# Rope by one copy and four transfers, a later split of the meta columns, and output weights placed earlier, in a hybrid attention layer

## The chip, the cores and the metric

The kernel runs on one core of a Trainium2 chip. The metric is the device time of one execution in microseconds (us), median of several runs. The core has five engines that each work through an instruction queue of their own in order: PE (TensorE, the matmuls; its weight loads are shown as PEld), DVE (VectorE), ACT (ScalarE), POOL (GpSimd) and SP (SyncE). In this kernel SP issues nearly all DMA transfers. An engine waits for another through semaphores.

## The reference

One decoder layer, float32, on 2048 tokens of width 1024 with 16 learned meta tokens ahead of them. Two attention branches run side by side on the same normalised input.

```python
xn = rms_norm(h, norm_gain[l])
proj = xn @ w_in[l]
sb_q, sb_k, sb_v, sw_q, sw_k, sw_v, sb_z, sw_z, g_sb, g_sw = jnp.split(proj, offsets, axis=-1)
o_sb = stick_breaking_attention(sb_q, sb_k, sb_v, valid)          # 8 heads of 64
q = rope(sw_q, pos)                                               # 16 heads of 64
k = rope(sw_k, pos)                                               # 2 heads of 64
o_sw = sliding_window_sink_attention(q, k, sw_v, attn_sinks[l], valid)   # window 128
y_sb = (o_sb * jax.nn.silu(sb_z)) @ w_branch_sb[l]
y_sw = (o_sw * jax.nn.silu(sw_z)) @ w_branch_swa[l]
merged = jax.nn.sigmoid(g_sb) * y_sb + jax.nn.sigmoid(g_sw) * y_sw
h = h + merged @ w_out[l]
return rms_norm(h, final_norm_gain)[:, BLOCK:]
```

The shapes of the heads are left out. `rope` takes each head's 64 values as two halves x1 and x2 and returns x1·cos − x2·sin and x2·cos + x1·sin: each half needs its partner half, 32 positions away.

## The kernel before

**Layout and splitting.** Activations lie transposed: features on the 128 partitions, tokens along the row in groups of 512 (four groups). To keep float32 accuracy each operand of a projection is held as a high and a low part, and a product is three matmuls (L461: xh·wh, xl·wh, xh·wl); a tile of 128 features by 512 tokens is 24 such matmuls over the eight 128-rows of the depth. The low part of a weight tile is `wl`, a subtraction on DVE (L119), stored to memory for the second use of the same weights by SP (`l_in_w_in<-wl`).

**Stages.** The work runs in two halves, groups 2 and 3 and then groups 0 and 1. In the profile the first sliding-window stage lies at about 60 to 372 us, the first stick-breaking stage at 372 to 562 us, a stage of gate products at 562 to 776 us, the second sliding-window stage at 776 to 1080 us, the second stick-breaking stage at 1080 to 1600 us, and `finish` (branch projections, merge, output projection, last norm) from 1600 us to the end.

**Who sets the order.** PE's instructions run in the order in which the program writes them: `weave` mixes the projection tiles with the units of attention by a clock of estimated costs. The other engines and SP are ordered by a scheduler from its own timeline, except in a hand-ordered stretch at the start, which ends at `hand.close()`.

**The sliding-window stage.** `window` builds key tiles (`sw_k`, L687 and L689 spread them over `kk`), value tiles (`sw_v`) and query tiles (`sw_q`). A key or query tile that comes out of PE in a PSUM bank goes through `rope` (L675 to L679): ACT copies each 32 rows to the place of their partner rows (four activations of 32x512, lines 675 and 676, `u`); DVE multiplies the bank itself by the cosines (L677, `t`), then `u` by the sines (L678), and adds (L679). A query tile is then split into high and low parts (`put_q`: casts on ACT at L736, subtractions on DVE at L737). One attention unit is: scores on PE (L756), copies and masks (L759, L760), maximum (L762), exponentials (L764), scaling (L765, L766); three units later the weights are transposed on PE (L790), split into `ph` (ACT) and `pl` (DVE) by `evac_split` (L126, L127), POOL selects `pm` from both (L796), PE multiplies with the values (L812), and ACT and DVE write the output (L814, L818). Value differences `xs` are moved between partitions with 64 KB transfers inside the core (`xs<-xs`). Every tile named `tmp` comes from one ring of nine.

**The stick-breaking stage.** `row` makes a row of scores (L915), a sigmoid (L918) and a running product (L923, L925); `turn` transposes rows (L944). POOL gathers the last 16 columns, those of the meta tokens, in `mr` (L931), and ACT and DVE split them into `m` (L934, L935), which `turn_meta` uses later.

**Finish.** `out_weights(k, ch)` loads a 128x512 piece of the output weights (`a<-in_w_out`), and splits it (L269 on ACT, L270 on DVE) into two tiles of the ring `ringr`, which has 32. The first column half (`ch` 0) is made inside the loop over `d`, piece `d` at the end of step `d`; the second half is made while the output products (L333 to L335) run.

Of the kernel before, what the change touches and what calls it, by code (L numbers as in the profile page):

```python
# [8 lines left out]
F32R = mybir.dt.float32r  # L9
I32 = mybir.dt.int32  # L10
AF = mybir.ActivationFunctionType
ALU = mybir.AluOpType
# [4 lines left out]
P = 128  # L17
# [3 lines left out]
NM = 16  # L21
GT = 512
# [21 lines left out]
def f32(ap):  # L44
    return ap.bitcast(F32)
# [3 lines left out]
def tile_kernel(ctx, tc, x, xt, meta, metat, gain, w_in, w_sb, w_sw, w_out, sinks, fgain,  # L49
# [8 lines left out]
    def DMA(dst, src):  # L58
        nc.sync.dma_start(*(t.bitcast(F32) if t.dtype == F32R else t for t in (dst, src)))
# [47 lines left out]
    msd = [dram(f"msd{p}", [NM, P]) for p in range(2)]  # L107
    vsv = dram("vsv", [P, 2 * P], F32R)

    vsplit, hsplit = [False], [True]  # L110

    def split(h, l, src):

# [121 lines left out]
    def finish(ringl, osw, first):  # L235
# [4 lines left out]
            return ps("gzt"[next(banks) % 3])  # L240

        def ringr(dt=F32R):
            return cp.tile([P, GT], dt, tag="R", name="ringr", bufs=32)

        def small(tag, bufs):
            return cp.tile([P, GT], F32, tag=tag, name=tag, bufs=bufs)
# [15 lines left out]
        for half, groups in enumerate(halves):  # L262
# [12 lines left out]
            for d, g in order:  # L275
                if d == 3 and g == groups[0]:
                    osb = {(k, g): gated(od, zs, k, g, ringr, lambda: small("a", AB)) for g in groups for k in range(4)}
                if d not in ws_of:
                    ws_of[d] = first if half == d == 0 else weights(d * P, w_sw)
                ws = ws_of[d]  # L280
                acc = bank()
                project(acc, ws, [osw[k, g] for k in range(8)])
                gt = small("gt", 3)
                DMA(gt, gw[d][g])
                part[d, g] = ringr(F32)
                V.tensor_tensor(part[d, g], acc, gt, op=ALU.mult)
            for d in range(8):
                ws = weights(d * P, w_sb)
                for g in groups:
                    acc = bank()  # L290
                    project(acc, ws, [osb[k, g] for k in range(4)])
                    gt = small("gt", 3)
                    DMA(gt, gs[d][g])
                    V.tensor_tensor(gt, acc, gt, op=ALU.mult)
                    V.tensor_tensor(gt, gt, part[d, g], op=ALU.add)  # L295
                    mh, ml = merged[d, g] = ringl(), ringl()
                    A.copy(mh, gt)  # L297
                    V.tensor_tensor(ml, gt, f32(mh), op=ALU.subtract)
                out_weights(d, 0)
            for g in groups:  # L300
                for t0 in range(0, 4, 2):
                    res, ssq, scaled_by = {}, {}, {}
# [82 lines left out]
            tp.tile(shape, F32, tag=tag, name=tag, bufs=n)  # L385

    def tmp(dt=F32, rows=P):
        return tp.tile([rows, GT], dt, tag="tmp", name="tmp", bufs=9)

    def ring_x(dt=F32):  # L390
        return tp.tile([P, GT], dt, tag="xs", name="xs", bufs=XS)
# [256 lines left out]
    def window(half, groups, sp):  # L648
# [22 lines left out]

        def rope(acc, c, s, t, u, scale):

            for o in range(0, P, 64):
                A.activation(u[o:o + 32], acc[o + 32:o + 64], AF.Copy, scale=scale)  # L675
                A.activation(u[o + 32:o + 64], acc[o:o + 32], AF.Copy, scale=scale)
            V.scalar_tensor_tensor(t, acc, scale, c, op0=ALU.mult, op1=ALU.mult)  # L677
            V.tensor_tensor(u, u, s, op=ALU.mult)  # L678
            V.tensor_tensor(t, t, u, op=ALU.add)  # L679

# [169 lines left out]
    def stick(groups, bp):  # L850
# [45 lines left out]
        def row(h, g, n, j):  # L896

            if n == j == 0:
                load_kv(h, g)
                state[h, g] = {"q": load_q(h, g), "last": {}}  # L900
            st = state[h, g]
            last = st["last"]
            b0 = 4 * (g + n) + j
            nb = min(4, NB - b0)
            end = b0 + nb == NB
            w = nb * P + (NM if end and nb < 4 else 0)
            k0 = (b0 - 4 * groups[0]) * P
            pieces = [("z", 0, w)]
            if end and nb == 4:
                pieces = [("z", 0, w // 2), ("z", w // 2, w // 2 + NM)]  # L910
                w += NM
            banks = [ps(tag) for tag, _, _ in pieces]
            for t, qt in enumerate(st["q"]):
                for z, (_, c, m) in zip(banks, pieces):
                    T.matmul(z[:, :m], lhsT=qt[:, j * P:(j + 1) * P], rhs=kt[h][:, k0 + c:k0 + c + m], start=t == 0, stop=t == 1)  # L915
            r = bp.tile([P, RW], F32, tag="row", name="row", bufs=12)
            for z, (_, c, m) in zip(banks, pieces):
                A.activation(r[:, c:c + m], z[:, :m], AF.Sigmoid, scale=-1.0)  # L918
            if n == 0 and mask is None:
                G.affine_select(out=r[:, :P], in_=r[:, :P], pattern=[[1, P]], compare_op=ALU.is_ge,  # L920
                                fill=1.0, base=-1, channel_multiplier=-1)
            if n == 0 and mask is not None:
                V.tensor_tensor_scan(r[:, :w], r[:, :w], mask[:, :w], 1.0, op0=ALU.mult, op1=ALU.max)  # L923
            else:
                V.tensor_tensor_scan(r[:, :w], r[:, :w], r[:, :w], last[j] if n else 1.0, op0=ALU.mult, op1=ALU.min)  # L925
            last[j] = r[:, w - 1:w]
            rows_of[h, g, n, j] = r
            if end:
                if j == 0:
                    st["mr"] = bp.tile([P, 4, NM], F32, tag="mr", name="mr", bufs=2)  # L930
                G.tensor_copy(st["mr"][:, j], r[:, w - NM:w])  # L931
                if j == 3:
                    m = st["m"] = bp.tile([P, 4, 2, NM], F32R, tag="m", name="m", bufs=2)
                    A.copy(m[:, :, 0], st["mr"])  # L934
                    V.tensor_tensor(m[:, :, 1], st["mr"], f32(m[:, :, 0]), op=ALU.subtract)  # L935

        def turn(h, g, n, i):

            i = 3 - i if n == 0 else i
            nr = i + 1 if n == 0 else 4  # L940
            tr = ps("t")
            for j in range(nr):
                k0 = (i - j) % 4 * P
                T.transpose(tr[:, j * P:(j + 1) * P], rows_of[h, g, n - (j > i), j][:, k0:k0 + P], ident)  # L944
            m = nr * P
            wh = bp.tile([P, GT], F32R, tag="wh", name="wth", bufs=3)
            wl = bp.tile([P, GT], F32R, tag="wl", name="wtl", bufs=3)
            evac_split(wh[:, :m], wl[:, :m], tr[:, :m])
            av_todo.append((h, g, vc[h, g + n][:, i, :], wh[:, :m], wl[:, :m], n == 0 and i == 3, False))

        def turn_meta(h, g):
            p, a = divmod(h, 2)
# [31 lines left out]
        for s in range(n + lt + 3):  # L984
            if s < n:
                row(*steps[s])
                yield 0.45 if s >= lt else 1.31
            t = s - lt
            if 0 <= t < n:
                turn(*steps[t])  # L990
                turned.append(s)
                yield 0.43
                h, g, step, i = steps[t]
                if g + step == 3 and i == 1:
                    turn_meta(h, g)
                    yield 0.11
                if g + step == i == 3:
                    av_todo.append((h, g, vm[:, h // 2, h % 2, :], wm[g % 2], None, False, True))
                    turned.append(s)
            while av_todo and turned[0] < s - 1:  # L1000
                del turned[0]
                yield values()
# [341 lines left out]
    for half, groups in enumerate(halves):  # L1344
        gts = [lambda spec=spec: gate(*spec) for spec in specs[half]]
        with tc.tile_pool(name=f"swa{half}", bufs=1, side="left") as sp:
# [19 lines left out]
            if m:  # L1366
                (wk, use_k, _), (wv, use_v, _), (wq, use_q, _) = sw_k(), sw_v(), sw_q(0)
                hold[0] = True
                drain(col_tile(wk, g0, use_k), col_tile(wv, g0, use_v), col_tile(wq, g0, use_q, bank="z"))
                flush(waiting)  # L1370
                drain(lagged(col_tile(wk, g1, use_k, True, "o", "t")))
                hold[0] = False
                meta_k = pending[:]
                del pending[:]
                drain(col_tile(wv, g1, use_v, True, "z", "t"))
                pending.append(lambda: flush(waiting))
                back = tp.tile([P, GT], F32, tag="rb", name="back", bufs=1)
                for i in range(2):
                    sums_back.append(back[:NM, i * P:(i + 1) * P])
                    DMA(sums_back[i], msd[i])  # L1380
                hand.close()
                vsplit[0] = False
                drain(tiles_by_tile(q[0][1:], groups[:1]))
                vsplit[0] = True
                late.extend(meta_k)
                pending.append(lambda: pending.extend(held))
            else:
                for mk, gs_ in ((sw_k, groups), (sw_v, groups), *((f, groups[:1]) for f in q[0])):
                    w, use, _ = mk()
                    for g in gs_:  # L1390
                        drain(lagged(col_tile(w, g, use, bank=("g", "z")[len(begun) % 2])))
                        begun.append(g)
# [120 lines left out]
```

## Time and profile before

| | |
|---|---|
| three runs, us | 2091.18, 2091.21, 2091.5 (median 2091.21) |
| the profiled execution, its own time | 2093.26 us |
| its span in the profile | 2091.2 us |
| granted clock of TensorE | 0.999 |
| instructions | 30957 |

The profile is of one execution. The page gives for each engine its busy time and how many instructions it ran. A row of the view of groups reads: line, engine, operation, output<-input, shape and count, then busy time, mean ns of one, and the idle time of the engine just before these instructions with what ended it. A row of the waits reads: engine, output, line <- what ended the wait, then us in total, times, and the longest. A row of the timeline reads: start, duration, engine, line, operation, tiles, shape, and in brackets the idle time before it with its releaser; neighbours of one kind are joined (x2, x4). A row of stages reads: from and to, length, then busy time and count of PE, PEld, DVE, ACT and POOL, the granted clock, the busy share of the DMA engines, and GB/s.

### The profile page before, as it was taken

How to read it: one execution, taken by the hardware profiler on the slowest of the kernel's cores; microseconds unless marked ns; L12 is line 12 of the kernel's file. 1: busy time of each engine (PE TensorE's matmuls, PEld its weight loads, DVE VectorE, ACT ScalarE, POOL GpSimd, SP SyncE). 2: the span in 40 equal slices, each digit the busy share in tenths (PEclk: the TensorE clock that was granted, in tenths of full speed). 3: DMA queues.
4: the chain of work that ended last, by engine and by line, in shares of the span. 5: the costliest groups of instructions: out<-in, count | busy, mean ns of one | idle time of the engine just before them, and what ended most of it. 6: DMA issues, size and time to landing. Idle time of an engine off the chain costs nothing.

```text
span 2091.2 us, 30957 instructions
## 1 busy us (share of the span) xinstructions
PE 2075.8 (99%) x10579; PEld 1743.0 (83%) x10579; DVE 1461.4 (70%) x2383; ACT 1091.0 (52%) x2657; POOL 343.5 (16%) x682
## 2 busy tenths in 40 slices
PE   9999999999999999999999999999999999999998
PEld 7888888888888888888888888888888888788887
DVE  7897986877687754888728888777774547464553
ACT  6677774577665335777735555655653202320121
POOL 1233444331000000333310000000000343000000
PEclk9999999999999999999999999999999999999999
DMA  9855545866287574435455444343424986568522
GB/s 335 323 187 195 192 171 181 253 201 185 87 291 292 201 257 154 159 131 172 151 176 161 120 131 128 113 131 94 125 84 168 359 303 219 186 228 303 154 96 91
DMA packets 170094, 391.48 MB, mean 187 GB/s; under 512 B 23728, under 2 KB 28208, under 8 KB 169936
## 3 DMA queue, kind: packets, MB, share of 16 engines
q1 hardware_dynamic: 169648, 389.23, 55.5%
q8 instruction: 84, 1.38, 0.3%
q14 instruction: 74, 0.61, 0.1%
q10 hardware_dynamic: 288, 0.27, 0.0%
HBM read 241.68 MB, written 145.18 MB: 185 GB/s over the span
## 4 chain that ended last, share of the span: by engine, by line
PE 90%; DVE 4%; ACT 3%; DMA 1%; issue 1%; POOL 1%; SPq 0%; DVEq 0%; ACTq 0%; POOLq 0%
PE ps_g L461 39%; PE ps_o L970 6%; PE ps_z L915 6%; PE ps_t L944 6%; PE ps_z L756 3%; PE ps_o L812 2%; PE ps_g L259 1%; PE ps_g L260 1%; PE ps_g L258 1%; PE ps_t L790 1%; PE ps_z L260 1%; PE ps_z L259 1%; PE ps_z L258 1%; PE ps_t L259 1%; PE ps_t L260 1%; PE ps_t L258 1%
## 5 line engine op out<-in xcount | busy, mean ns | idle before, releaser
L461 PE MATMUL ps_g<-xh,wh 128*128 128x512 f32 x1264 | 516.1, 408 | 0.8 <-DVE tmp L677 0.6
L461 PE MATMUL ps_g<-xl,wh 128*128 128x512 f32 x1264 | 495.1, 392 | 0.7 <-DVE xl L1192 0.6
L461 PE MATMUL ps_g<-xh,wl 128*128 128x512 f32 x1264 | 494.9, 392 | 0.4 <-DVE wl L119 0.4
L925 DVE TENSOR_TENSOR_SCAN row<-row 128x512 f32<-128x512 f32 (+4 forms) x256 | 290.2, 1134 | 116.1 <-POOL row L920 60.0
L461 PEld LDWEIGHTS ps_g<-xh,wl 128*128 128x128 f32 x1264 | 237.3, 188 | 53.3 <-DVE wl L119 0.8
L461 PEld LDWEIGHTS ps_g<-xh,wh 128*128 128x128 f32 x1264 | 238.1, 188 | 39.4 <-ACT xh L1191 1.2
L461 PEld LDWEIGHTS ps_g<-xl,wh 128*128 128x128 f32 x1264 | 238.6, 189 | 38.3 <-DVE xl L1192 2.0
L918 ACT ACTIVATE row<-ps_z 128x512 f32<-128x512 f32 (+4 forms) x352 | 174.8, 508 | 159.5 <-PE ps_z L915 155.1
L127 DVE SCALAR_TENSOR_TENSOR wtl<-ps_t,wth 128x512 fp32r<-128x512 f32 (+1 forms) x320 | 188.8, 590 | 21.3 <-ACT wth L126 20.7
L126 ACT ACTIVATE wth<-ps_t 128x512 fp32r<-128x512 f32 (+1 forms) x320 | 171.6, 536 | 61.6 <-PE ps_t L944 59.8
L915 PE MATMUL ps_z<-kt,q 128*128 128x512 f32 (+4 forms) x704 | 183.6, 349 | 2.2 <-ACT row L918 2.2
L944 PE MATMUL ps_t<-ident,row 128*128 128x128 f32 x1088 | 171.4, 273 | 1.0 <-DVE wtl L127 0.8
L944 PEld LDWEIGHTS ps_t<-ident,row 128*128 128x128 f32 x1088 | 134.6, 140 | 33.0 <-DVE wtl L127 1.8
L915 PEld LDWEIGHTS ps_z<-kt,q 128*128 128x128 f32 x704 | 124.4, 188 | 27.6 <-ACT row L918 5.3
L970 PE MATMUL ps_o<-wth,vc 128*128 128x512 f32 (+1 forms) x320 | 131.3, 410 | 0.0
L970 PE MATMUL ps_o<-wtl,vc 128*128 128x512 f32 (+1 forms) x320 | 116.4, 364 | 0.0
L764 ACT ACTIVATE sc<-sc,nm 128x129 f32<-128x129 f32 x256 | 100.0, 393 | 29.9 <-DVE nm L762 29.1
L931 POOL COPY mr<-row 128x16 f32<-128x16 f32 x128 | 28.3, 223 | 444.6 <-DVE row L925 401.9
L612 ACT ACTIVATE tmp<-ps_g 128x512 f32<-128x512 f32 x80 | 47.9, 599 | 83.6 <-PE ps_g L461 77.3
L297 ACT CAST ringl<-gt 128x512 fp32r<-128x512 f32 x32 | 19.9, 622 | 128.5 <-DVE gt L295 127.6
L117 POOL TENSOR_SCALAR wh<-raw 128x1024 fp32r<-128x1024 f32 (+1 forms) x45 | 50.2, 1116 | 215.7 <-PE ps_g L461 49.8
L923 DVE TENSOR_TENSOR_SCAN row<-row,mask 128x512 f32<-128x512 f32 (+2 forms) x64 | 70.0, 1100 | 17.7 <-ACT row L918 17.1
(442 smaller groups left out, 4211.6 us busy)
## 6 DMA issues: line engine op xcount, KB each, us to landing
wh<-h_in_w_in SPq DMA_DIRECT2D x66, 512.0 KB, 3.9
wl<-l_in_w_in SPq DMA_DIRECT2D x66, 512.0 KB, 5.1
h_in_w_in<-wh SPq DMA_DIRECT2D x50, 512.0 KB, 3.1
l_in_w_in<-wl SPq DMA_DIRECT2D x50, 512.0 KB, 4.1
raw<-in_w_in SPq DMA_DIRECT2D x49, 512.0 KB, 5.1
q<-qd SPq DMA_DIRECT2D x128, 128.0 KB, 3.1
vc<-vd SPq DMA_DIRECT2D x48, 256.0 KB, 3.1
kd<-tmp SPq DMA_DIRECT2D x32, 256.0 KB, 3.3
```

The source lines that it names most:

```text
L126: A.activation(h, acc, AF.Copy, scale=scale)
L127: V.scalar_tensor_tensor(l, acc, scale, f32(h), op0=ALU.mult, op1=ALU.subtract)
L258: T.matmul(acc, lhsT=wh[:, k, :], rhs=h, start=k == 0, stop=False)
L259: T.matmul(acc, lhsT=wh[:, k, :], rhs=l, start=False, stop=False)
L461: T.matmul(acc, lhsT=a[:, k, :], rhs=b[:, k, :], start=k == i == 0, stop=k == KT - 1 and i == 2)
L764: A.activation(sc[:, hh, :], sc[:, hh, :], AF.Exp, bias=nm[:, hh:hh + 1], accum_out=den[:, hh:hh + 1])
L915: T.matmul(z[:, :m], lhsT=qt[:, j * P:(j + 1) * P], rhs=kt[h][:, k0 + c:k0 + c + m], start=t == 0, stop=t == 1)
L918: A.activation(r[:, c:c + m], z[:, :m], AF.Sigmoid, scale=-1.0)
L923: V.tensor_tensor_scan(r[:, :w], r[:, :w], mask[:, :w], 1.0, op0=ALU.mult, op1=ALU.max)
L925: V.tensor_tensor_scan(r[:, :w], r[:, :w], r[:, :w], last[j] if n else 1.0, op0=ALU.mult, op1=ALU.min)
L944: T.transpose(tr[:, j * P:(j + 1) * P], rows_of[h, g, n - (j > i), j][:, k0:k0 + P], ident)
L970: T.matmul(o[:, :n], lhsT=v, rhs=r, start=first and r is wh, stop=last)
```

## The change

Three edits. In `rope`, after the hand-ordered stretch, ACT makes one scaled copy of the whole tile into a further `tmp` tile, four transfers on SP's queue put its 32-row pieces into `u` beside their partners, and the product with the cosines reads the copy. The first three ropes (inside the hand-ordered stretch) keep the old form. The ring of `tmp` grows from 9 to 11. In the stick-breaking stage the split of the meta columns moves in the program from the last row to a step of its own, one turn ahead of `turn_meta`. In `finish` the pieces of the first column half of the output weights are made two steps of `d` earlier, and `ringr` grows from 32 to 40.

```diff
-    vsplit, hsplit = [False], [True]
+    vsplit, hsplit, turn_hand = [False], [True], [True]
...
-            return cp.tile([P, GT], dt, tag="R", name="ringr", bufs=32)
+            return cp.tile([P, GT], dt, tag="R", name="ringr", bufs=40)
...
                 V.tensor_tensor(part[d, g], acc, gt, op=ALU.mult)
+            for d in range(2):
+                out_weights(d, 0)
             for d in range(8):
                 ws = weights(d * P, w_sb)
...
-                out_weights(d, 0)
+                if d < 6:
+                    out_weights(d + 2, 0)
...
-        return tp.tile([rows, GT], dt, tag="tmp", name="tmp", bufs=9)
+        return tp.tile([rows, GT], dt, tag="tmp", name="tmp", bufs=11)
...
         def rope(acc, c, s, t, u, scale):
 
-            for o in range(0, P, 64):
-                A.activation(u[o:o + 32], acc[o + 32:o + 64], AF.Copy, scale=scale)
-                A.activation(u[o + 32:o + 64], acc[o:o + 32], AF.Copy, scale=scale)
-            V.scalar_tensor_tensor(t, acc, scale, c, op0=ALU.mult, op1=ALU.mult)
+            if turn_hand[0]:
+                for o in range(0, P, 64):
+                    A.activation(u[o:o + 32], acc[o + 32:o + 64], AF.Copy, scale=scale)
+                    A.activation(u[o + 32:o + 64], acc[o:o + 32], AF.Copy, scale=scale)
+                V.scalar_tensor_tensor(t, acc, scale, c, op0=ALU.mult, op1=ALU.mult)
+            else:
+                a = tmp()[:, :t.shape[1]]
+                A.activation(a, acc, AF.Copy, scale=scale)
+                for o in range(0, P, 64):
+                    DMA(u[o:o + 32], a[o + 32:o + 64])
+                    DMA(u[o + 32:o + 64], a[o:o + 32])
+                V.tensor_tensor(t, a, c, op=ALU.mult)
             V.tensor_tensor(u, u, s, op=ALU.mult)
             V.tensor_tensor(t, t, u, op=ALU.add)
...
-                if j == 3:
-                    m = st["m"] = bp.tile([P, 4, 2, NM], F32R, tag="m", name="m", bufs=2)
-                    A.copy(m[:, :, 0], st["mr"])
-                    V.tensor_tensor(m[:, :, 1], st["mr"], f32(m[:, :, 0]), op=ALU.subtract)
...
+        def split_meta(h, g):
+            st = state[h, g]
+            m = st["m"] = bp.tile([P, 4, 2, NM], F32R, tag="m", name="m", bufs=2)
+            A.copy(m[:, :, 0], st["mr"])
+            V.tensor_tensor(m[:, :, 1], st["mr"], f32(m[:, :, 0]), op=ALU.subtract)
...
                 h, g, step, i = steps[t]
+                if g + step == 3 and i == 0:
+                    split_meta(h, g)
                 if g + step == 3 and i == 1:
                     turn_meta(h, g)
...
                 hand.close()
+                turn_hand[0] = False
                 vsplit[0] = False
```

## Prediction

> **What bounds the kernel now.** I read the first part of the page, then TensorE's waits, then the table of busy times by stage.
>
> ```profile
> span 2091.2 us, 30957 instructions
> PE 2075.8 (99%) x10579; PEld 1743.0 (83%) x10579; DVE 1461.4 (70%) x2383; ACT 1091.0 (52%) x2657; POOL 343.5 (16%) x682
> PE ps_z L915 <- ACT row L918: 2.2, 3, 1.2
> ...
> PE ps_z L334 <- DVE ringr L270: 0.6, 3, 0.2
> PE ps_g L461 <- DVE tmp L677: 0.6, 1, 0.6
> ...
> PE ps_g L461 <- DVE wl L119: 0.4, 1, 0.4
> PE ps_z L756 <- DVE sc L760: 0.3, 1, 0.3
> PE ps_z L756 <- DVE q L737: 0.2, 1, 0.2
> PE ps_o L812 <- POOL pm L796: 0.2, 1, 0.2
> 60.00:372.00 312.00, 311.14 (x1747) 265.57 (x1746) 259.24 (x502) 210.97 (x598) 123.22 (x215) 1.00 0.59 206
> ...
> 776.00:1080.00 304.00, 302.81 (x1621) 259.99 (x1620) 209.28 (x426) 208.31 (x570) 75.51 (x164) 1.00 0.45 153
> ```
>
> TensorE (PE) is idle for 2091.2 − 2075.8 = 15.4 us of the span. Its order of instructions is written by hand and the change leaves all of it as it is, so the change can only shorten or lengthen PE's waits. The rope rewrite lives in the two sliding-window stages, the last two rows (span of the stage, then busy PE, PEld, DVE, ACT, POOL). PE idles there for 0.86 and 1.19 us in all; DVE is busy for 259 of 312 us in the first and 209 of 304 us in the second, ACT for 211 and 208. So there is next to nothing to win in these stages, and DVE in the first is the helper with least room. The gain that all three edits can reach is bounded by the waits that name their lines: L677, L756 twice, L812, L119, L915 and L334, 4.5 us together.
>
> **Rope, its work.** 34 of 37 ropes change (the first three keep the old form): 33 of 128x512 and the one of 128x16 for the meta tokens.
>
> ```profile
> L675 ACT ACTIVATE tmp<-ps_g 32x512 f32<-32x512 f32 x64 | 37.8, 590 | 11.2 <-PE ps_g L461 10.0
> L676 ACT ACTIVATE tmp<-ps_g 32x512 f32<-32x512 f32 x64 | 37.7, 588 | 0.8
> L612 ACT ACTIVATE tmp<-ps_g 128x512 f32<-128x512 f32 x80 | 47.9, 599 | 83.6 <-PE ps_g L461 77.3
> L677 DVE SCALAR_TENSOR_TENSOR tmp<-ps_g,ct 128x512 f32<-128x512 f32 x32 | 22.1, 691 | 35.4 <-ACT tmp L676 35.1 <-DMA vd<-tmp 0.2
> L678 DVE TENSOR_TENSOR tmp<-tmp,sn 128x512 f32<-128x512 f32 x36 | 25.0, 694 | 0.0
> xs<-xs SPq DMA_DIRECT2D x32, 64.0 KB, 2.0
> L59 SPq DMA_DIRECT2D xs<-xs x16: 461/478/548, 829.7 to 971.1; - x16
> DMA to landing us min/median/max: 1.9/2.0/3.9
> ```
>
> Four shifted ACT copies (2 x 0.590 + 2 x 0.588 = 2.36 us) give way to one full copy; L612 is the same operation and shape, 0.60 us. ACT saves 1.76 us per rope, 33 x 1.76 = 58 us of 1091, all of it beside PE's work. DVE's product with the cosines reads SBUF instead of PSUM: 0.694 (L678's form) for 0.691, nothing. Added are 4 x 34 = 136 transfers on SP's queue. The nearest rows are the 64 KB copies xs<-xs, also memory to memory inside the core: some 0.48 us of SP for each issue (the three figures are ns, least, median, most) and 2.0 us from issue to landing, 3.9 at worst. Four issues one behind the other and one landing make 3 x 0.5 + 2.0 = 3.5 us, so from the start of the copy to the product with the sines (L678) pass 0.6 + 3.5 = 4.1 us. Before it was 2.36 + 0.69 = 3.05 us. **A rope gets about 1.1 us later in a free queue**, 3.0 us later with the worst landing; if the pieces overlap better, the lower end is 0.6 + 1.9 − 3.05 = −0.5.
>
> The new wait is L678's, for four transfers. DVE works in order, so behind it stand the sum L679, the masks and maxima of the scores (L760, L762), the output products L818, weight splits L119 and above all the split `pl` (L127), for which POOL's L796 and then PE's L812 wait. In the built order three or four of these now come between the cosine and the sine product, which hides most of the wait; before, DVE waited 35.1/32 = 1.1 us per rope at L677 in the same way. In general I set this at zero, and look at the places where PE has no margin.
>
> **Place 1, the weight split at 80 us.**
>
> ```profile
> 78.61 1.42 DVE L679 TENSOR_TENSOR tmp<-tmp 128x512 f32<-128x512 f32 x1
> 80.07 2.53 ACT L687 CAST kk<-tmp 64x512 fp32r<-64x512 f32 x4 [3.85 <-DVE tmp L679]
> 80.16 1.20 DVE L119 TENSOR_TENSOR wl<-raw,wh 128x1024 fp32r<-128x1024 f32 x1
> 80.65 0.39 PE L461 MATMUL ps_g<-xl,wh 128*128 128x512 f32 x1
> 81.42 0.50 PE L461 MATMUL ps_g<-xh,wl 128*128 128x512 f32 x1 [0.38 <-DVE wl L119]
> ```
>
> PE waits for `wl` already. In the new order two of the subtractions L689 stand ahead of this L119. They need the casts L687, which end 0.63 us apart from 80.07 on; the second subtraction ends near 80.07 + 1.27 + 0.7 = 82.0 (L678's size of operation), and the split at 83.2 instead of 81.4. PE: **+1.8 us**. Bounds: 0 if the casts come sooner, 2.5 if the subtractions wait for all of ACT's queue.
>
> **Place 2, the last query tile of the first half.**
>
> ```profile
> 309.21 0.69 DVE L127 SCALAR_TENSOR_TENSOR pl<-ps_t,ph 128x512 fp32r<-128x512 f32 x1
> 309.94 1.50 DVE L737 TENSOR_TENSOR q<-tmp,q 64x512 fp32r<-64x512 f32 x2
> 311.49 0.50 PE L756 MATMUL ps_z<-kk,q 128*128 128x256 f32 x2 [0.25 <-DVE q L737]
> ```
>
> No margin here either: PE starts as soon as L737 has ended at 311.44. In the new order the sum L679, a 511-column subtraction, a softmax product and two small operations come between `pl` and L737: from 309.9 on, three full-size operations by L678's 0.69 and some 0.4 for the small ones, 2.5 us, and then 1.5, so L737 ends near 313.9 at the latest and near 313.0 if the small ones and half an operation overlap; I take 313.4. PE: **+1.9 us**. Bounds: −0.25 (the wait goes) and +3.0 (worst landing).
>
> **Place 3, a values unit at 177 us.**
>
> ```profile
> 171.84 1.23 DVE L119 TENSOR_TENSOR wl<-raw,wh 128x1024 fp32r<-128x1024 f32 x1
> 173.09 0.32 SPq L59 DMA_DIRECT2D l_in_w_in<-wl  x1
> 175.67 0.68 DVE L127 SCALAR_TENSOR_TENSOR pl<-ps_t,ph 128x512 fp32r<-128x512 f32 x1
> 176.88 0.28 PE L812 MATMUL ps_o<-pl,vv 128*128 128x256 f32 x1
> ```
>
> PE reads `pl` half a microsecond after its end at 176.35. In the new order this `pl` is queued behind a sine product, and three of that rope's four transfers stand in SP's queue behind the store of `wl`, which cannot issue before the split L119 has ended (173.09). They issue near 174 to 175 and land near 177, so `pl` would end near 178.3 and PE lose 1.4 us. Whether this rope and this split keep their places in time I can't tell: between 0 and 1.9 I take **+0.7**.
>
> **What the rope gives back.**
>
> ```profile
> 832.12 0.59 ACT L675 ACTIVATE tmp<-ps_g 32x512 f32<-32x512 f32 x1
> 834.06 0.39 PE L461 MATMUL ps_g<-xl,wh 128*128 128x512 f32 x1
> 834.28 0.39 PE L461 MATMUL ps_g<-xh,wl 128*128 128x512 f32 x1
> 835.29 0.50 PE L461 MATMUL ps_g<-xh,wh 128*128 128x512 f32 x1 [0.62 <-DVE tmp L677]
> ```
>
> Here PE wants the bank that four ACT copies and L677 still read. The new rope frees a bank after one copy, at 832.12 + 0.6 = 832.7. Matmuls follow at 0.22 us (834.06, 834.28), so of 1.01 us from start to start 0.8 go: **−0.8 us**. The wait L812 for `pm` (0.2) is of the same kind, with `ph` behind four ACT copies: −0.2.
>
> **Later split of the meta columns.**
>
> ```profile
> 484.84 0.25 ACT L934 CAST m<-mr 128x64 fp32r<-128x64 f32 x1 [0.54 <-POOL mr L931]
> 485.68 0.63 PE L915 MATMUL ps_z<-kt,q 128*128 128x400 f32 x2 [0.45 <-ACT row L918]
> ```
>
> On ACT and DVE this small cast and its subtraction come in the same place as before in 31 of 32 cases; the scheduler had put them there already. The exception is the one shown, where it moves behind one ACT copy and L918 comes 0.25 us sooner: −0.25 us, 0 to −0.45.
>
> **Output weights sooner.**
>
> ```profile
> 1782.16 8.05 SPq L59 DMA_DIRECT2D a<-in_w_out  x8
> 1787.03 0.62 ACT L269 CAST ringr<-a 128x512 fp32r<-128x512 f32 x1 [3.23 <-DMA a<-in_w_out]
> ```
>
> PE's wait in the finish (L334 for L270) falls on these eight transfers, the second column half of the output weights. The edit moves the first half, and SP's order around these eight stays. So nothing: 0 to −0.6. The eight added slots and the earlier casts lie beside matmuls on engines that are idle for most of the finish.
>
> **Sum.** 1.8 + 1.9 + 0.7 − 0.8 − 0.2 − 0.25 = +3.15, say +3 us. The profiled execution is 2093.26 us (2.06 more than its span); it would be 2096.3. The runs' median is 2.05 lower than it, 2091.21: **2094.2 us**, +0.14%.
>
> **Rival A, slower: transfers behind weight loads.**
>
> ```profile
> wl<-l_in_w_in SPq DMA_DIRECT2D x66, 512.0 KB, 5.1
> ```
>
> In the new order of SP many ropes' four transfers come straight behind a pair of 512 KB weight loads. If they land late with them, at the 3.9 us of the worst copy rather than 2.0, or later, L678 is 1.9 us or more later and DVE's queue with it. Place 3 shows units with half a microsecond of margin; if 5 of the 16 ropes of the first half hit such a unit, that is 5 x (1.9 − 0.5) = 7 us more: 2101 us. For it: DVE has 53 us of room over 16 ropes there, and L812's wait row shows that margins reach zero. Against: the median of 2.0 us was measured among the same loads. It decides from landings of about 3 us on. The Trainium skill (DMA: Bandwidth & Descriptors, section "Queues, rings and completion order") says that each DMA engine consumes its descriptors in ring order, and by that rule such a piece would land no sooner than the loads ahead of it, 5.1 us by the row above, so 3.1 later and 5 x 2.6 = 13 us more. The trace bears it out at most in part, by the 3.9 beside the 2.0.
>
> **Rival B, shorter: the relief is all that counts.** Places 1 to 3 keep their times, because casts come sooner or the queue has room, and the waits for L677, L812, L760, L756 and L915 go: −0.8 − 0.2 − 0.3 − 0.25 − 0.45 = −2.0, 2089.2 us. For it: ACT loses a fifth of its work in both stages. Against: at places 1 and 2 the order itself has changed. Below 2087 it would take waits that no row ties to these lines.
>
> **Rival C, nothing:** the split stays where it was, the finish waits for the other half, and ropes have margin: 2091.2 us.
>
> **How the numbers follow.** About 0.2% (4.2 us: under 2087.0 or over 2095.4) is what a measurement of this kernel tells from no change. Forecast 0.48, of which a quarter lies over 2095.4 (its own range is 2091.5 to 2097, from the bounds of places 1 to 3); A 0.28; B 0.14, with 0.04 below 2087; C 0.10. Faster 0.04, same 0.36 + 0.10 + 0.10 = 0.56, slower 0.12 + 0.28 = 0.40. The range runs from B's 2089.2 to A's 2101.
>
> **What would show it.** ACT's busy time near 1033 us and DVE's unchanged; tmp<-tmp transfers x132 of 64 KB with a median near 2.0 to 2.5 (over 3: A); a PE wait for `wl` of some 2 us near 83 us; one for L737's successor of about 2 us near 313; L812 waiting for `pl` or `pm` near 178; none for the rope's cosine product near 835; PE's wait for L270 in the finish as before. Wrong would be the forecast if PE's waits in 60 to 372 us came to under 1 or over 8 us, or if the time moved in stages without a rope.

## The result and the profile after

The changed kernel takes 2110.86 us (median of 6 runs, 2107.77 to 2112.59) against 2091.56 us before (6 runs, 2091.18 to 2092.67): ratio 1.0088, 95% interval 1.0077 to 1.0098. It is 19.3 us slower, where no change clear of noise was forecast. The profiled execution took 2108.19 us with a span of 2106.1.

First part of the page, then TensorE's waits (us in total, times, longest), then SP's issues (KB each, us to landing), then two rows of the groups, of the changed kernel. Its lines are 3 to 15 further down than before: L464 is L461 of before, L767 L756, L823 L812, L748 L737; L684 is the new copy, L688 the product with the cosines, L689 that with the sines, L690 the sum.

```profile
span 2106.1 us, 31065 instructions
## 1 busy us (share of the span) xinstructions
PE 2079.4 (99%) x10579; PEld 1745.6 (83%) x10579; DVE 1462.0 (69%) x2383; ACT 1032.5 (49%) x2555; POOL 340.8 (16%) x682
```

```profile
PE ps_o L823 <- POOL pm L807: 3.9, 9, 1.1
PE ps_z L767 <- DVE q L748: 3.2, 4, 2.5
PE ps_o L823 <- DVE pl L127: 2.1, 2, 1.4
PE ps_g L464 <- DVE wl L119: 1.9, 1, 1.9
PE ps_z L767 <- DVE sc L771: 1.7, 2, 0.9
...
PE ps_t L596 <- DVE tmp L568: 1.4, 1, 1.4
...
PE ps_t L596 <- DVE tmp L591: 1.0, 1, 1.0
```

```profile
wl<-l_in_w_in SPq DMA_DIRECT2D x66, 512.0 KB, 5.3
...
tmp<-tmp SPq DMA_DIRECT2D x132, 64.0 KB, 3.5
```

```profile
L689 DVE TENSOR_TENSOR tmp<-tmp,sn 128x512 f32<-128x512 f32 x36 | 25.6, 711 | 43.8 <-DMA tmp<-tmp 43.6
...
L688 DVE TENSOR_TENSOR tmp<-tmp,ct 128x512 f32<-128x512 f32 x33 | 23.5, 713 | 7.0 <-ACT tmp L684 6.8
```

ACT did lose its work: 1091.0 − 1032.5 = 58.5 us. But PE now waits for all that hangs on DVE's queue in the two sliding-window stages: `pm` and `pl` (6.0 us together, 0.2 before), `q` (3.2, 0.2 before), masked scores (1.7, 0.3 before), and two pieces of the value tiles (L596). The pieces of the ropes land in 3.5 us in the median, not in 2.0, and DVE waits for them 43.6 us. One rope shows the whole chain. SP's, DVE's and PE's timelines of the changed kernel (start, duration, and in brackets the wait):

```profile
143.81 0.33 SPq L59 DMA_DIRECT2D wh<-h_in_w_in  x1
144.23 0.38 SPq L59 DMA_DIRECT2D wl<-l_in_w_in  x1
144.71 3.17 SPq L59 DMA_DIRECT2D tmp<-tmp  x4
```

```profile
150.18 0.87 DVE L777 TENSOR_TENSOR sc<-sc,den 128x512 f32<-128x512 f32 x1
152.43 0.69 DVE L689 TENSOR_TENSOR tmp<-tmp,sn 128x512 f32<-128x512 f32 x1 [1.38 <-DMA tmp<-tmp]
153.03 0.68 DVE L127 SCALAR_TENSOR_TENSOR pl<-ps_t,ph 128x512 fp32r<-128x512 f32 x1
```

```profile
152.14 0.28 PE L823 MATMUL ps_o<-ph,vv 128*128 128x256 f32 x1
153.77 0.38 PE L823 MATMUL ps_o<-pl,vv 128*128 128x256 f32 x1 [1.36 <-DVE pl L127]
154.64 0.38 PE L823 MATMUL ps_o<-pm,xs 128*128 128x256 f32 x1 [0.49 <-POOL pm L807]
```

Two weight loads of 512 KB are issued at 143.81 and 144.23, the rope's four pieces right behind them from 144.71 on. They take 5.2 to 7.2 us to land (the trace's view of the ring of tmp in this window, below), the last at 152.4. The sine product stands ahead of `pl` in DVE's queue, so `pl`, which could have followed L777 at 151.1, starts at 153.03, and PE loses 2.3 us in two steps (1.63 between the first two rows and 0.87 between the next, where before these matmuls were about 0.11 us apart).

```profile
DMA to landing us min/median/max: 5.2/6.5/7.2
```

Since PE's order is the same in both kernels, its n-th matmul of the one can be set against the n-th of the other. That gives, for the two profiled executions, where the delay of 15.7 us at the end arises: +1.5 at 81 us (the weight split), +2.7 at the two pieces of value tiles, +5.5 at four places where the scores of a unit start (2.0 of it waiting for masked scores, 3.5 for `q`, of which 2.7 at the last query tile of the first stage), +3.8 at `pl` and `pm` in the first stage and +4.0 in the second; −0.8, −0.5 and −0.4 at 835, 836 and 928 us, −1.3 in the finish, the rest in small steps. By stage, 13.9 us of delay arise from 60 to 372 us and 4.2 from 776 to 1080 us.

DVE's waits for ropes stand the other way round: they are shorter in the first stage than in the second. The rows give them for the first and then the second stage, of the kernel before (two rows) and of the changed kernel (two rows):

```profile
DVE tmp L677 <- ACT tmp L676: 8.5, 11, 1.8
DVE tmp L677 <- ACT tmp L676: 30.2, 18, 6.5
DVE tmp L689 <- DMA tmp<-tmp: 16.8, 9, 3.6
DVE tmp L689 <- DMA tmp<-tmp: 26.7, 12, 5.2
```

In the second stage the pieces land later (4.0 us in the median, 2.3 in the first) and DVE waits longer, yet PE loses less there. So neither the median landing nor the sum of DVE's waits gives the price by itself; what stands behind each wait must count too.

### The profile page after: what moved, and what is told of

The parts are those of the page before. It is cut to its first block, busy times and chain, and to the rows that moved or that the text cites. A ratio compares the mean times of both kernels' runs of the same rounds, so it can differ in the third digit from the quotient of the medians.

```text
span 2106.1 us, 31065 instructions
## 1 busy us (share of the span) xinstructions
PE 2079.4 (99%) x10579; PEld 1745.6 (83%) x10579; DVE 1462.0 (69%) x2383; ACT 1032.5 (49%) x2555; POOL 340.8 (16%) x682
## 4 chain that ended last, share of the span: by engine, by line
PE 84%; DVE 7%; ACT 3%; DMA 2%; issue 2%; POOL 1%; SPq 1%; DVEq 0%; ACTq 0%; POOLq 0%
PE ps_g L464 31%; PE ps_o L983 6%; PE ps_z L926 6%; PE ps_t L951 6%; DMA tmp<-tmp 2%; PE ps_z L464 2%; PE ps_g L259 1%; PE ps_g L260 1%; PE ps_g L258 1%; PE ps_z L259 1%; PE ps_z L260 1%; PE ps_z L258 1%; PE ps_z L767 1%; PE ps_o L823 1%; PE ps_t L259 1%
## 5 line engine op out<-in xcount | busy, mean ns | idle before, releaser
L464 PE MATMUL ps_g<-xh,wh 128*128 128x512 f32 x1264 | 516.9, 409 | 0.5 <-ACT xh L1206 0.5
L464 PE MATMUL ps_g<-xh,wl 128*128 128x512 f32 x1264 | 495.3, 392 | 1.9 <-DVE wl L119 1.9
L464 PE MATMUL ps_g<-xl,wh 128*128 128x512 f32 x1264 | 495.3, 392 | 0.7 <-DVE xl L1207 0.6
L464 PEld LDWEIGHTS ps_g<-xh,wl 128*128 128x128 f32 x1264 | 237.7, 188 | 55.2 <-DVE wl L119 2.3
L464 PEld LDWEIGHTS ps_g<-xl,wh 128*128 128x128 f32 x1264 | 238.9, 189 | 38.2 <-DVE xl L1207 1.8
L464 PEld LDWEIGHTS ps_g<-xh,wh 128*128 128x128 f32 x1264 | 238.5, 189 | 38.5 <-ACT xh L1206 1.4
L123 POOL TENSOR_TENSOR wl<-raw,wh 128x256 fp32r<-128x256 f32 x88 | 85.8, 1005 | 2.0
```

The costliest lines, as they stand in the source:

```text
L123: G.tensor_tensor(l[:, c], src[:, c], f32(h[:, c]), op=ALU.subtract)
L464: T.matmul(acc, lhsT=a[:, k, :], rhs=b[:, k, :], start=k == i == 0, stop=k == KT - 1 and i == 2)
```

## The experiments

The theory after the result, W: the four transfers land late, and DVE, which works in order, holds `pl`, masks and query splits of other units behind the product that needs them. Rivals: another part of the change, the traffic and SP's time for 136 transfers, the new order on DVE, the queue that the transfers go through. Each run stands beside runs of the kernel before on the same chip.

**Which edit.** The rope edit alone, put into the kernel before:

```diff
-            V.scalar_tensor_tensor(t, acc, scale, c, op0=ALU.mult, op1=ALU.mult)
...
+                a = tmp()[:, :t.shape[1]]
+                A.activation(a, acc, AF.Copy, scale=scale)
+                for o in range(0, P, 64):
+                    DMA(u[o:o + 32], a[o + 32:o + 64])
+                    DMA(u[o + 32:o + 64], a[o:o + 32])
+                V.tensor_tensor(t, a, c, op=ALU.mult)
...
-        return tp.tile([rows, GT], dt, tag="tmp", name="tmp", bufs=9)
+        return tp.tile([rows, GT], dt, tag="tmp", name="tmp", bufs=11)
...
+                turn_hand[0] = False
```

> Theory W (the rope's four transfers land late because they are issued behind pairs of 512 KB weight loads in SP's queue, and DVE, in order, holds everything behind the sine product): the rope edit alone carries the whole loss, 2110 to 2114 us, that is the changed kernel's 2110.9 plus the 1 to 2 us that the finish seems to give back. Rival S (the moved meta split or the larger ring of output weights takes part of it): under 2107 us.

Measured: 2111.16 us, ratio 1.0092 (1.0078 to 1.0106). The rope edit and its ring carry the whole loss. The other way round, the changed kernel with the old rope throughout:

```diff
-                turn_hand[0] = False
...
-        return tp.tile([rows, GT], dt, tag="tmp", name="tmp", bufs=11)
+        return tp.tile([rows, GT], dt, tag="tmp", name="tmp", bufs=9)
```

> The changed kernel with the old rope everywhere. Theory W: 2089.5 to 2091.5 us, a gain of 0.5 to 1.5 us from the waits near 1788 to 1792 us in the finish (three steps of 0.3 to 0.5 us there were gone in the changed kernel), nothing from the meta split. Rival S: over 2094 us.

Measured: 2091.43 us, ratio 0.9997 (0.9989 to 1.0006). The later meta split and the earlier output weights change nothing that the time can tell.

**The wait or the transfers.** The transfers are made, but the products read the unrotated copy:

```diff
+            if not turn_hand[0]:
+                V.tensor_tensor(t, t, s, op=ALU.mult)
+                V.tensor_tensor(t, t, a, op=ALU.add)
+                return
             V.tensor_tensor(u, u, s, op=ALU.mult)
```

> The changed kernel in which the transfers are made but not read: cosine and sine product and the sum use the unrotated copy, so the rotation by 32 rows is left out of keys and queries. Theory W: without the wait for landings DVE's queue runs free, 2089 to 2095 us. Rival T (the 136 transfers cost by their traffic and by the time SP spends issuing them, which delays weights and other loads): over 2100 us.

Measured: 2090.88 us, ratio 0.9991 (0.9982 to 1.0). With the same 136 transfers on SP's queue, landing in 3.6 us as before, 20 us are gone. Neither traffic nor SP's time costs anything that shows; what costs is that the products read the pieces. That takes in two things which this run does not part: DVE's wait for the landings, and DVE's order, which is another one here (at 144 us the sine product starts 1.2 us after the cosine product, in the changed kernel 6.1 us after it). SP's issues, then TensorE's waits of this kernel:

```profile
tmp<-tmp SPq DMA_DIRECT2D x132, 64.0 KB, 3.6
```

```profile
PE ps_g L464 <- DVE wl L119: 1.9, 1, 1.9
...
PE ps_z L771 <- DVE q L752: 0.4, 2, 0.2
```

No row for `pm` or `pl` is left, and the wait for `q` is 0.4. The one at `wl` stays, so it has another cause.

**Why they land late.** First another queue, ACT's, for the four pieces:

```diff
-                    DMA(u[o:o + 32], a[o + 32:o + 64])
-                    DMA(u[o + 32:o + 64], a[o:o + 32])
+                    A.dma_start(u[o:o + 32], a[o + 32:o + 64])
+                    A.dma_start(u[o + 32:o + 64], a[o:o + 32])
```

> The changed kernel with the rope's four transfers issued from ACT's queue instead of SP's; the weight loads stay with SP. Theory W: they no longer stand behind the loads, median landing falls from 3.5 to 2.0 to 2.6 us, DVE's idle time before the sine product from 43.6 to under 25 us, and the time to 2095 to 2103 us (ACT pays some 2 us of issue per rope, the order on DVE stays another one than before). Rival C (the DMA engines themselves are busy, whatever the queue): median landing stays at 3.3 us or more and the time at 2106 us or more.

Measured: 2119.0 us, ratio 1.0127 (1.0112 to 1.0143). The expectation of W fell: the pieces still land in 3.9 us. SP's, then ACT's timeline of one rope (the first and the last of its four issues), then the row of all pieces:

```profile
210.72 0.32 SPq L59 DMA_DIRECT2D wh<-h_in_w_in  x1
211.13 0.38 SPq L59 DMA_DIRECT2D wl<-l_in_w_in  x1
```

```profile
211.59 0.51 ACTq L686 DMA_DIRECT2D tmp<-tmp  x1
...
213.42 0.60 ACTq L687 DMA_DIRECT2D tmp<-tmp  x1
```

```profile
tmp<-tmp ACTq DMA_DIRECT2D x132, 64.0 KB, 3.9
```

Nothing stands ahead of the pieces in ACT's queue, and this rope's took 4.3 to 5.5 us all the same. So it is not the order within a queue. The time is 8 us longer than with SP, although DVE's wait for the pieces falls from 43.6 to 32.0 us. ACT is held for 2.3 us per rope by the issues, and DVE's order is another one too (about 230 of its 1378 instructions from 60 to 1100 us stand elsewhere in the queue); which of the two costs the 8 us was not tried. The Trainium skill (DMA: Bandwidth & Descriptors, section "Issuing engines are not separate DMA queues") says that transfers started by ScalarE, SyncE or GpSimd run on the same 16 DMA engines and interleave. This run agrees for SyncE and ScalarE, with 3.9 us beside 3.5.

Then the weight loads themselves. Each stored tile of the input projection is loaded to one eighth, and PE uses that eighth eight times:

```diff
+            if w is w_in:
+                wh, wl = wh[:, 0:1, :], wl[:, 0:1, :]
             for t, k in zip((wh, wl), kept[key]):
-                DMA(t, k)
+                DMA(t, k[:, 0:t.shape[1]])
...
-                T.matmul(acc, lhsT=a[:, k, :], rhs=b[:, k, :], start=k == i == 0, stop=k == KT - 1 and i == 2)
+                T.matmul(acc, lhsT=a[:, k % a.shape[1], :], rhs=b[:, k, :], start=k == i == 0, stop=k == KT - 1 and i == 2)
```

> The changed kernel with each stored weight tile of the input projection loaded to one eighth (64 KB instead of 512 KB); PE uses that eighth for all eight, so the projections of those tiles are left wrong in value. Issue counts and all other transfers are as in the changed kernel. Theory C (the pieces land late since the DMA engines are still at work on 1 MB of weights issued just before, on whichever queue): median landing of the pieces falls from 3.5 to 2.0 to 2.3 us, DVE's idle time before the sine product from 43.6 to under 25 us, the time to 2093 to 2100 us. Rival I (the pieces are slow by themselves or by their own queue): landing stays over 3 us, and the time at 2106 us or more.

Measured: 2097.97 us, ratio 1.0029 (1.0017 to 1.0042). SP's issues, then DVE's wait at the sine product (the waits' row) of this kernel:

```profile
tmp<-tmp SPq DMA_DIRECT2D x132, 64.0 KB, 2.0
```

```profile
DVE tmp L691 <- DMA tmp<-tmp: 24.5, 18, 3.4
```

With the same number of issues in the same queue the pieces land in 2.0 us, DVE's wait for them falls from 43.6 to 24.5 us, and 12.9 of the 20 us are gone. DVE's order is nearly that of the changed kernel (about 50 of those 1378 instructions stand elsewhere). So the pieces land late because up to 1 MB of weights, issued just before, is still under way, and about 12.9 us of the loss come from it. What small loads would do to the kernel before was not run, but no wait of its PE names a weight load. In the second stage, where no raw weights are loaded any more, the loss is gone, and the gains of 0.8, 0.5 and 0.4 us remain. What is left (6 us over before) lies in the first stage, where raw weights and stores of 512 KB still run; there 8.5 of the 13.9 us stay, though the pieces land in 2.0 us in the median: +1.5 at 81 us, +1.1 at a value tile, +0.5 and +0.3 at `pm`, +1.0 at masked scores, +0.8 and +2.1 at query tiles. Some of those ropes' pieces are issued late. SP's timeline in the changed kernel (the copy of this rope ended at 237.4):

```profile
238.28 2.53 SPq L59 DMA_DIRECT2D vm<-vm  x2
240.90 1.05 SPq L59 DMA_DIRECT2D vd<-tmp  x2
242.04 1.15 SPq L59 DMA_DIRECT2D tmp<-tmp  x2
```

The pieces stand behind four transfers of a value tile; 4.6 us pass between copy and first issue. How the rest divides between this and the order on DVE was not taken apart.

**Where it costs.** The new rope in the second stage only:

```diff
             if not m:
+                turn_hand[0] = False
                 ts = [mk() for mk in sbt[:3]]
...
                 hand.close()
-                turn_hand[0] = False
```

> The new rope only in the second sliding-window stage (17 of 34), the old one before. Theory W2 (late landings cost where DVE has little room and query tiles are needed soon, which is the first stage): the second stage adds 2 to 4 us, 2093 to 2096 us. Rival H (each late rope costs the same, about 20/34 = 0.6 us): 2101 us.

Measured: 2094.86 us, ratio 1.0012 (1.0003 to 1.0021). 18 ropes (not the 17 of the expectation), more than half, give 3.2 us, and 1.5 of these arise at 81 us in the first stage, where no rope has changed in this kernel. Their pieces land in 4.2 us in the median and DVE waits 25.8 us for them, yet the second stage adds only 1.5 us to the profiled execution. So the first stage bears most of the loss. Its DVE had been busy for 259 of 312 us before, against 209 of 304 in the second; that this is the reason fits W2 and was not tried by itself.

**Ask for query tiles later.** `QW` from 6 to 10:

> The changed kernel with QW at 10 instead of 6, so that PE's hand-written order asks for a query tile some 4 us of its clock later. Theory W3 (about half of the loss comes through query tiles that are ready too late): 2100 to 2105 us. Rival V (it comes through the split of transposed weights, held in DVE's queue behind the sine product): 2107 us or more.

Measured: 2119.48 us, ratio 1.0125 (1.0111 to 1.0139). PE's wait for `q` is out of the list, but `pl` and `pm` make 7.4 us, and at the start of the stick-breaking stage PE waits 6.3 us for loads of `q` from memory. The profiled execution, 2113.15 us, is the fastest of four, so it does not show all of the loss; but even less these 6.3 us it lies over the 2105 us of W3. W3 fell: asking later moves the wait on. It fits V, but since PE's own order changes too, it does not show V.

**Another mover.** POOL copies in place of the transfers:

```diff
-                    DMA(u[o:o + 32], a[o + 32:o + 64])
-                    DMA(u[o + 32:o + 64], a[o:o + 32])
+                    G.tensor_copy(u[o:o + 32], a[o + 32:o + 64])
+                    G.tensor_copy(u[o + 32:o + 64], a[o:o + 32])
```

> The changed kernel with the four pieces moved by POOL copies of 32x512 instead of transfers; same result. Theory C: what hurts is the unsteady landing, and four POOL copies of about 0.6 us each take about as long as the four ACT copies before: 2089 to 2094 us. Rival P (any detour of the rope over a further engine costs, since POOL's copies stand ahead of the selections that PE waits for): 2098 us or more.

Measured: 2123.9 us, ratio 1.0149 (1.0136 to 1.0163). Rows of the groups of this kernel:

```profile
L686 POOL COPY tmp<-tmp 32x512 f32<-32x512 f32 x66 | 58.7, 889 | 86.2 <-DMA qd<-tmp 38.6 <-ACT tmp L684 18.5 <-DVE vv L127 13.5
...
L687 POOL COPY tmp<-tmp 32x512 f32<-32x512 f32 x66 | 50.5, 766 | 2.7
```

A copy takes 0.77 to 0.89 us, four 3.3 us, and selections for `pm` stand behind them: at 332 us one waits until four copies have run (from 327.68 to 331.5), and PE waits 3.9 us for it. PE's waits for `pm` and `pl` come to 13.5 us. The rival holds: the steady mover is no better if its queue is one that PE's values hang on.

**The step at 81 us.** The kernel before with the larger ring alone:

```diff
-        return tp.tile([rows, GT], dt, tag="tmp", name="tmp", bufs=9)
+        return tp.tile([rows, GT], dt, tag="tmp", name="tmp", bufs=11)
```

> The kernel before with the ring of tmp tiles at 11 instead of 9 and nothing else. Theory R (the larger ring alone moves the weight split L119 behind the key subtractions at 80 us, since the stall of 1.5 us there also shows in the run that keeps the old rope in the first stage): 2092.5 to 2094 us, with a step of about 1.5 us in PE's start at 81 us and no other over 0.5. Rival N (the ring changes nothing by itself): 2091 to 2092 us and no such step.

Measured: 2094.73 us, ratio 1.0013 (1.0004 to 1.0022). DVE's, then PE's timeline of this kernel:

```profile
79.72 1.38 DVE L689 TENSOR_TENSOR kk<-tmp,kk 64x512 fp32r<-64x512 f32 x2 [0.50 <-ACT kk L687]
81.14 1.23 DVE L119 TENSOR_TENSOR wl<-raw,wh 128x1024 fp32r<-128x1024 f32 x1
```

```profile
80.12 0.40 PE L461 MATMUL ps_g<-xl,wh 128*128 128x512 f32 x1
82.41 0.50 PE L461 MATMUL ps_g<-xh,wl 128*128 128x512 f32 x1 [1.89 <-DVE wl L119]
```

Two more slots for `tmp`, and not one instruction more: the scheduler puts the weight split behind two subtractions, and PE waits 1.89 us for it instead of 0.38. The time is 2.6 us longer, over R's range. The profiled run had a second step, 1.3 us in the finish, which R had excluded; there PE's waits for the output weights come and go by 0.3 to 0.5 us in most runs, and no run ties this step to the ring.

**The new rope at two places.** The old rope, the ring of 9, the other two edits, and the new rope only for two query tiles of the second stage:

```diff
+                turn_hand[0] = (half, p, g) not in ((1, 0, groups[1]), (1, 4, groups[0]))
                 rope(acc, ct[:, cols(n)], sn[:, cols(n)], t, tmp(), 0.125)
+                turn_hand[0] = True
```

> The old rope everywhere but at two query tiles of the second stage, those whose four ACT copies PE waits for at 835 and 928 us; the meta split and the finish as in the changed kernel, the ring of tmp at 9. Theory W: three steps of 0.8, 0.5 and 0.4 us go and no landing is late enough to be missed there, 2089.3 to 2090.5 us. Rival D (another order on DVE around these ropes takes it back): 2091 us or more.

Measured: 2090.34 us beside 2092.17 us for the kernel before, ratio 0.999 (0.9981 to 0.9999). The wait for `ps_g` at 835 us is gone, as the PE timeline shows (833.76 and 833.98 are the same two matmuls as 834.28 and 835.29 before), and the row under it is DVE's wait for the pieces:

```profile
833.76 0.39 PE L464 MATMUL ps_g<-xh,wl 128*128 128x512 f32 x1
833.98 0.39 PE L464 MATMUL ps_g<-xh,wh 128*128 128x512 f32 x1
```

```profile
DVE tmp L689 <- DMA tmp<-tmp: 1.2, 2, 0.8
```

DVE waits 1.2 us for the pieces in all. Used where PE waits for the bank and nothing waits for the rope, the edit gains 1.3 us there (0.8 and 0.5); the third step that W named, 0.4 us at 928 us, did not come (0.05). The rest of the time's 1.8 us is spread over other places, and the interval just excludes no change.

## Why the prediction was wrong

**The step that failed** is the one that set the general cost of the new wait at zero. It rested on a landing of 2.0 us, read from the copies xs<-xs, and on three or four DVE instructions that would hide what is left. But those copies mostly have no weight load just ahead of them. Three of their sixteen pairs were issued within 1.3 us behind one, and these landed in 2.7 to 3.9 us in the kernel before already. The 3.9 us that the prediction takes for the worst copy are such a case. SP's timeline of the kernel before, and the landing of the two copies:

```profile
828.06 0.32 SPq L59 DMA_DIRECT2D wh<-h_in_w_in  x1
828.47 0.39 SPq L59 DMA_DIRECT2D wl<-l_in_w_in  x1
829.75 1.13 SPq L59 DMA_DIRECT2D xs<-xs  x2
```

```profile
DMA to landing us min/median/max: 3.4/3.6/3.9
```

The ropes' pieces often stand there: they land in 3.5 us in the median, and in 5.2 to 7.2 in the rope shown. From the end of the copy to the last landing 3.9 us pass in a free queue (the rope at 1001 us, near the 3.5 of the estimate), but 7.7 us at 144 us. The comparison with the wait at L677, 1.1 us per rope, was a mean over two stages, and the first had 8.5 us of it where the new wait is 16.8. The sum had three places and 3 us; the run that does not read the pieces shows 20 us for all that hangs on reading them. PE's waits in 60 to 372 us come to 12.4 us, over the 8 that the prediction had named as a sign of being wrong.

**What the 20 us are made of.** 12.9 us go when the weight loads are small. The other 7 lie in the first stage, in DVE's new order and in pieces that are issued late; how they divide stays open. The ring's step of 1.5 us at 81 us and the gains of 1.7 us are in both kernels and come on top.

**The range** of the forecast, 2091.5 to 2097, is said to come from the bounds of places 1 to 3. Its upper end does (2097.4 with all of them high), its lower end does not: with all of them low the sum gives 2089.7.

**Rival A** was the right mechanism, late landings and DVE's queue behind them, and its sign, a median over 3 us, came true over both stages (in the first stage alone it is 2.3). Its argument against, that the 2.0 us "was measured among the same loads", was wrong, as the copies at 829.75 show. Its price of 7 us was too small, and it counted ropes of the first half alone: in the profiled executions small loads take 5.3 us off the first stage and 6.4 off the second. Its place, SP's queue, is wrong too, since the pieces land as late from ACT's. The figure by ring order, 13 us in place of 7, lies near the 12.9 by luck: the five units were assumed for the first stage, half of the gain lies in the second, and order in SP's ring cannot be the whole reason, with ACT's queue as late.

**Place 1** was right in its size (+1.5 measured, 1.8 forecast) and its order on DVE, and wrong in its owner: it belongs to the ring of 11, not to the ropes. **Place 2**: +2.7 against 1.9; the order named is what ran. DVE's and PE's timelines of the changed kernel:

```profile
322.03 0.68 DVE L690 TENSOR_TENSOR tmp<-tmp 128x512 f32<-128x512 f32 x1
...
322.72 0.66 DVE L564 TENSOR_TENSOR tmp<-tmp,ps_g 128x511 f32<-128x511 f32 x1
...
323.50 0.67 DVE L777 TENSOR_TENSOR sc<-sc,den 128x512 f32<-128x512 f32 x1
324.20 1.40 DVE L748 TENSOR_TENSOR q<-tmp,q 64x512 fp32r<-64x512 f32 x2
```

```profile
325.03 0.47 PE L767 MATMUL ps_z<-kk,q 128*128 128x256 f32 x2 [2.52 <-DVE q L748]
```

Pieces of that rope landed in 2.0 us, and with small loads most of the step stays (+2.1 of +2.7), so here it is the order and not the landing. **Place 3**: +0.3 against 0.7, within its bounds. **Given back**: the bank −0.8 as forecast, the scores after it −0.5, which were only in rival B, `pm` −0.4 against 0.2. **ACT** saved 58.5 us against 58, and DVE's busy time stayed (1461.4 and 1462.0), as forecast. **Meta split**: −0.26 us at 485.7 us, as forecast (−0.25). The step is there in every profiled kernel with the later split and in none of the two without it (rope edit alone, ring alone), but it is too small for the times to show. **Finish**: nothing in the time, as forecast; single waits of 0.3 to 0.5 us come and go from run to run. That the engines beside PE are idle for most of the finish holds for ACT (105 of 491 us busy before), not for DVE (252).

## What to carry to other kernels

A transfer that a tight stage waits for is to be priced by what is issued just ahead of it, from SP's queue or from ACT's, and not by the median of like transfers elsewhere; their worst case may be the one that counts. An engine that works in order passes a wait on to everything behind it: ask whose inputs stand behind the waiting instruction, not only who uses its output. And relief for an engine that is half idle, 58 us of ACT here, is worth only the waits that name it, 1.7 us.

## What the runs showed of the hardware that was not expected

The transfers of 32x512 take SP 0.58 us each in the median to issue, and moving them to ACT's queue does not shorten their landing (3.9 against 3.5 us). A 64 KB copy inside the core lands in 2.0 us in the median with small weight loads around it and in 3.5 us with loads of 512 KB. A POOL copy of 32x512 float32 takes 0.77 to 0.89 us within SBUF, where ACT takes 0.59 from PSUM. Enlarging a ring of buffers, with no instruction added, cost about 1.5 us at one weight split through the scheduler's order (2.6 us by the medians of the runs).
